# Query and key products with both parts of x in 512 columns, and other places for a loop's margin and a residual

## The chip, the cores and the metric

One core of a Trainium2 chip runs the whole kernel. The metric is the device time of one execution in microseconds, taken as the median of several runs. Durations of single instructions come from one profiled execution. TensorE multiplies, VectorE and ScalarE work on tiles, GpSimd makes masks and constants, and SyncE issues all loads and stores.

## The reference

One decoder layer works on 256 tokens of 2048 features in float32. Attention comes first: `qkv = x @ w_qkv` (2048 x 6144), 16 heads of 128, a causal softmax with a distance penalty over the one block of 256 keys, then `o @ w_o`. The sum `ALPHA * x + attention` goes through a LayerNorm. Then comes a mixture of 32 experts in four groups: each token takes one group and two experts of it, `silu(x @ w_gate) * (x @ w_up)`, weighted, and `@ w_down` (512 hidden features per expert). A second residual sum and a LayerNorm end the layer:

```
x = layer_norm(ALPHA * x + moba_attention(x, w_qkv, w_o), ln1)
x = layer_norm(ALPHA * x + hierarchical_moe(x, ...), ln2)
```

Only one key block exists at this length, so the selection of past blocks adds nothing. The expert weights are 32 x 3 matrices of 4 MB; the kernel reads all of them.

## The kernel before, in words

**Numbers.** For the query, key, value and output products each float32 operand is split in a high part, rounded to the format fp32r, and the rest as a low part. A product is the sum of high x high, high x low and low x high. `transpose_x` turns two chunks of 128 features of x over TensorE into PSUM, and ScalarE copies them to `xh` as the high part, VectorE subtracts to make `xl`. `split_w` does the same for half of a loaded weight tile: ScalarE rounds (L152), VectorE subtracts (L153). Three slots hold split weights, in turn.

**Attention.** `project(g)` makes q, k and v of four heads, `head` the softmax and the values of one head. In q and k the weights of a head are the stationary operand and 256 columns of `xh` or `xl` stream past them; `mm3` writes the three products into the head's half of a PSUM bank (L162 to L164). In v, x is stationary and 512 weight columns stream. A part loads four tiles of 1 MB into a ring of seven slots. After the part, two PSUM banks of 512 columns are copied out, q with the factor 1/sqrt(128) on VectorE (L198), k and v on ScalarE (L200, L202). Two pairs of banks alternate. Only the first part, q of group 0, has its order on TensorE, ScalarE and VectorE written out by hand (`first_order`); behind it the framework orders these engines, and it sets the heads of group g among the products of group g + 1. The first loads on SyncE's queue are a block of x (512 features, two loads) and a tile of weights in turn.

**Experts.** TensorE and SyncE follow the program's order here, and so do the others. Experts go in pairs p = 0 to 15, with up to 64 tokens each. In a pair `first_products` makes gate and up products for one expert after the other, in eight groups of 16 products (`gate_up`, four per expert); after each group `used` gives back two weight slots and issues the next loads into free slots (`advance`), and `between(p, i)` adds small jobs. Then `gather` picks the next pair's tokens, and `second_products` makes the down products in PSUM banks 4 to 7 (`yb`). The rows of pair p are added to the accumulator `acc` in `between` of pair p + 1, groups 0 to 3, over the same four banks (`rest`). Eighteen weight slots are in turn; the order of loads is pair by pair, gate and up (16 MB), then down (8 MB). The last pairs differ: the down weights of pair 14 come after the gate and up weights of pair 15, and those of pair 15 come last, by columns. SyncE waits at each load for one of eight DMA semaphores and for its slot.

**The loop.** After pair `LOOP_AFTER = 10` comes `further_passes`, a loop that serves experts with more than 64 tokens; its count is read from the data and is zero for this input, but all engines meet at its entry (L621) and its exit. Ahead of it, pair 10 keeps `LOOP_SLOTS = 4` slots free for the loop's body; behind it, `advance` fills all free slots.

**The residual.** `residual(n)` adds ALPHA times the normalised x, times gain plus bias, to 512 columns of `acc`. It runs in pair `RES_AT = 12`, once after each of groups 4 to 7 (counted from 0). `rows_of` spreads a vector over the partitions with four small products, into a bank of `mb`, which holds two; three such rows are needed per visit: the gain for either half of the tokens, which VectorE multiplies in place, and the bias.

Of the kernel before, what the change touches and what calls it, by code (L numbers as in the profile page):

```python
# [9 lines left out]
F32 = mybir.dt.float32  # L10
F32R = mybir.dt.float32r
# [3 lines left out]
ALU = mybir.AluOpType  # L15
AX = mybir.AxisListType

P = 128
D = 2048
NT = 2  # L20
NCH = D // P
# [34 lines left out]
def hybrid_kernel(ctx: ExitStack, tc: tile.TileContext, x, w_qkv, w_o, ln1_g, ln1_b, w_grp, b_grp,  # L56
# [68 lines left out]
    nc.scalar.activation(warm, zeros[:, 0:1], AF.Exp)  # L125


    xh = [slot(s, [P, 8, 256], f"xh{i}", F32R) for i, s in enumerate(S_XH)]
    xl = [slot(s, [P, 8, 256], f"xl{i}", F32R) for i, s in enumerate(S_XL)]
    tb = Rot([4, 5, 6, 7])  # L130

    def transpose_x(c2):
        pt = bank(tb(), [P, 2, 256], f"xt{c2}")
        for cc in range(2):
            for tt in range(NT):
                c = 2 * c2 + cc
                nc.tensor.transpose(pt[:, cc, tt * P:(tt + 1) * P], xs[tt][:, c * P:(c + 1) * P], ident)
        i, k = divmod(2 * c2, 8)
        nc.scalar.copy(xh[i][:, k:k + 2, :], pt)
        nc.vector.tensor_sub(xl[i][:, k:k + 2, :], pt, xh[i][:, k:k + 2, :].bitcast(F32))  # L140


    ws = Rot(S_WS)

    def split_w(wt, half, name, pieces=1):

        nch, width = wt.shape[1:]
        t = slot(ws(), [P, 2, nch // 2, width], name, F32R)
        src = wt[:, half * nch // 2:(half + 1) * nch // 2, :]
        for i in range(pieces):  # L150
            c = slice(i * nch // 2 // pieces, (i + 1) * nch // 2 // pieces)
            nc.scalar.copy(t[:, 0, c], src[:, c])  # L152
            nc.vector.tensor_sub(t[:, 1, c], src[:, c], t[:, 0, c].bitcast(F32))  # L153
        return t

    accb = Rot([0, 1, 2, 3])
# [4 lines left out]
    def mm3(dst, ah, al, bh, bl, start, stop, **kw):  # L161
        nc.tensor.matmul(dst, ah, bh, start=start, stop=False, **kw)  # L162
        nc.tensor.matmul(dst, ah, bl, start=False, stop=False, **kw)  # L163
        nc.tensor.matmul(dst, al, bh, start=False, stop=stop, **kw)  # L164

    def first_order():
        return tc.manual_schedule(engines={mybir.EngineType.Activation, mybir.EngineType.DVE, mybir.EngineType.PE})

    def project(g):
        qk = slot(S_QK[g % 2], [P, 2, 4, 256], f"qk{g}")  # L170
        v = vall[:, g % 2]
        for part in range(3):
            with first_order() if g == part == 0 else nullcontext():
                ps = [bank(accb(), [P, 512], f"pj{g}_{part}_{i}") for i in range(2)]
                if g == part == 0:
                    transpose_x(0)
                for j in range(4):
                    wt = first[j] if g == 0 and part == 0 else load_w(w_qkv, j, part * D + g * 512, 512, f"w{g}_{part}_{j}")
                    for half in range(2):
                        w2 = split_w(wt, half, f"ws{g}_{part}_{j}_{half}", 2 if g == part == j == 0 else 1)  # L180
                        if g == part == 0 and (j, half) != (3, 1):
                            transpose_x(2 * j + half + 1)
                        for cc in range(2):
                            c = 4 * j + 2 * half + cc
                            i, k = divmod(c, 8)
                            st, sp = c == 0, c == NCH - 1
                            if part < 2:
                                for hh in range(4):
                                    w = w2[:, :, cc, hh * P:(hh + 1) * P]
                                    mm3(ps[hh // 2][:, (hh % 2) * 256:(hh % 2 + 1) * 256], w[:, 0], w[:, 1], xh[i][:, k, :],  # L190
                                        xl[i][:, k, :], st and hh % 2 == 0, sp and hh % 2 == 1, skip_group_check=True)
                            else:
                                for tt in range(NT):
                                    t = slice(tt * P, (tt + 1) * P)
                                    mm3(ps[tt], xh[i][:, k, t], xl[i][:, k, t], w2[:, 0, cc, :], w2[:, 1, cc, :], st, sp)
            for i in range(2):
                if part == 0:
                    nc.vector.tensor_scalar_mul(qk[:, 0, 2 * i:2 * i + 2, :].rearrange("p a b -> p (a b)"), ps[i], SCALE)  # L198
                elif part == 1:
                    nc.scalar.copy(qk[:, 1, 2 * i:2 * i + 2, :].rearrange("p a b -> p (a b)"), ps[i])  # L200
                else:
                    nc.scalar.copy(v[:, i, :], ps[i])  # L202
        return qk, v

    sb = Rot([4, 5])
# [381 lines left out]
    def residual(n):  # L587

        cs = slice(n * 512, (n + 1) * 512)
        for tt in range(NT):  # L590
            g_ = rows_of(0, n, mb(), f"g1_{n}_{tt}")
            g4 = g_.rearrange("p (a c) -> p a c", c=4)
            nc.vector.scalar_tensor_tensor(g4, xn[tt][:, n].rearrange("p c a -> p a c"), ALPHA, g4, op0=ALU.mult, op1=ALU.mult)  # L593
            nc.vector.tensor_add(acc[tt][:, cs], acc[tt][:, cs], g_)  # L594
        b_ = rows_of(1, n, mb(), f"b1_{n}")
        for tt in range(NT):
            nc.vector.tensor_add(acc[tt][:, cs], acc[tt][:, cs], b_)

    def gates():
# [75 lines left out]

    def first_products(p):

        keep = LOOP_SLOTS if p == LOOP_AFTER else 0
        gu = [bank(gub(), [P, 512], f"gu{p}_{i}") for i in range(2)]
        hs = sm.tile([P, 512], F32, name=f"hs{p}", tag="ptv")  # L680
        for side in range(2):
            e = 2 * p + side
            for j in range(4):
                gate_up(gu[side], side, lambda c: xg[:, c, side], j, held["g", e, j], held["u", e, j])
                used(("g", e, j), ("u", e, j), keep=keep)
                between(p, 4 * side + j)
            if side == 0:
                o2_next = onehots(p + 1) if p + 1 < NP else None
                ot, gs = slots_of(p, o2, gatef[:, :, 2 * p:2 * p + 2])
            hidden(gu[side], side, gs, hs)  # L690
        return hs, ot, o2_next

    def second_products(p, ht):
        y = [bank(yb[n], [P, 512], f"y{p}_{n}") for n in range(4)]
        for k in range(4):
            for n in range(4):
                for side in range(2):
                    nc.tensor.matmul(y[n][sides[side]], ht[:, k, sides[side]], held["d", 2 * p + side, k][:, n * 512:(n + 1) * 512],  # L698
                                     start=k == 0, stop=k == 3, skip_group_check=True)
            used(("d", 2 * p, k), ("d", 2 * p + 1, k), keep=LOOP_SLOTS if p == LOOP_AFTER else 0)  # L700
        return y

    def between(p, i):

        nonlocal gatef
        if p == 0 and i < 2:
            for c2 in (2 * i + 4, 2 * i + 5):
                gather(c2, xg, o2, 0)
        if p == 0 and i == 1:
            gatef = gates()  # L710
            count_passes()
        if i < 4 and rest is not None:
# [187 lines left out]
```

## Time and profile before

| | us |
|---|---|
| median of three runs (1388.09 to 1393.47) | 1391.52 |
| profiled execution | 1390.78 |
| its span, first to last instruction | 1389.0 |
| TensorE busy | 1332.3 (96%) |
| VectorE busy | 462.7 (33%) |
| ScalarE busy | 334.7 (24%) |

The mean granted clock of TensorE is 0.986. Attention with its output product reaches to about 420 us, the experts from there to about 1350. Busy time of TensorE is modelled and overlaps from product to product, so the distance between starts tells more than a duration. A row of the page's second part has 40 slices of 34.7 us. In groups of instructions the number after the busy time is the mean of one in ns, then comes idle time ahead and what ended it. In a timeline the columns are start, duration, engine, line, operation, operands and count, with the idle time ahead in brackets. The chain of waits has start, duration, engine, tile, line and count.

### The profile page before, as it was taken

To read this page: it belongs to the slowest core of one execution; us is meant where nothing else is said; L and a number is where in the kernel's file an instruction comes from. 1 tells how busy PE (TensorE), PEld (TensorE's weight loads), DVE (VectorE), ACT (ScalarE), POOL (GpSimd) and SP (SyncE) were. 2 spreads that over 40 slices of the span, in tenths; PEclk is the share of its full clock that TensorE was granted. 3 is DMA by queue.
4 is the path that set the end of the run, shared out by engine and by line. 5 is a ranking of instruction groups with operands and counts; after the bars stand their busy time and mean duration, and the time that the engine had idled before them with its cause. 6 is when DMAs were issued, how large, how long until landed. Compare 5 with 4: busy or idle time off the path is not lost. (4 is left out here: it accounts for less than half of the span.)

```text
span 1389.0 us, 17892 instructions
## 1 busy us (share of the span) xinstructions
PE 1332.3 (96%) x7497; PEld 795.8 (57%) x7497; DVE 462.7 (33%) x814; ACT 334.7 (24%) x566; POOL 19.4 (1%) x58
## 2 busy tenths in 40 slices
PE   8999999999999999999999999999996997999996
PEld 8999898988896434534434344343443443443432
DVE  4454545545443122221221212212122026222146
ACT  4353534445334101101111011010111010111132
POOL 1000120000000000000000000000000000000000
PEclk9999999999999999999999999999998998999998
DMA  9745446477549899999999999999999999999992
GB/s 342 243 152 182 152 153 206 158 243 272 176 176 367 358 423 420 421 421 421 421 422 421 420 421 421 422 421 421 421 421 420 421 420 422 407 414 420 420 371 61
DMA packets 103015, 475.50 MB, mean 342 GB/s; under 512 B 12756, under 2 KB 18964, under 8 KB 54804
## 3 DMA queue, kind: packets, MB, share of 16 engines
q1 hardware_dynamic: 102932, 474.33, 86.3%
q8 instruction: 60, 0.98, 0.3%
q14 instruction: 23, 0.19, 0.0%
HBM read 472.20 MB, written 2.10 MB: 341 GB/s over the span
## 5 line engine op out<-in xcount | busy, mean ns | idle before, releaser
L543 PE MATMUL gu<-wg,xg 128*64 128x512 f32 x1024 | 460.4, 599 | 12.4 <-PEq L621 12.4
L543 PE MATMUL gu<-wu,xg 128*64 128x512 f32 x1024 | 460.9, 600 | 5.2 <-DMA wu<-in_moe_w_up_dram 5.2
L543 PEld LDWEIGHTS gu<-wg,xg 128*64 128x64 f32 x1024 | 135.2, 138 | 242.3 <-issue 235.3
L698 PE MATMUL y<-wd,ht 128*64 128x512 f32 x960 | 209.5, 594 | 0.8 <-ACT ht L555 0.8
L543 PEld LDWEIGHTS gu<-wu,xg 128*64 128x64 f32 x1024 | 135.1, 138 | 48.7 <-issue 37.4
L153 DVE TENSOR_TENSOR ws<-w,ws 128x1024 fp32r<-128x1024 f32 x88 | 108.2, 1230 | 121.7 <-ACT ws L152 121.7
L162 PE MATMUL pj<-xh,ws 128*128 128x256 f32 x512 | 147.1, 287 | 0.8 <-ACT ws L152 0.8
L164 PE MATMUL pj<-xh,ws 128*128 128x256 f32 x512 | 146.5, 287 | 1.0 <-DVE ws L153 1.0
L163 PE MATMUL pj<-xl,ws 128*128 128x256 f32 x512 | 146.8, 287 | 0.0
L510 PE MATMUL pg<-o,xn 128*128 128x128 f32 x1024 | 134.1, 286 | 11.8 <-ACT xg L519 6.1
L698 PEld LDWEIGHTS y<-wd,ht 128*64 128x64 f32 x960 | 68.7, 137 | 131.0 <-issue 127.1
L510 PEld LDWEIGHTS pg<-o,xn 128*128 128x128 f32 x1024 | 123.2, 195 | 33.3 <-issue 14.5
L576 DVE TENSOR_TENSOR acc<-acc,cb 128x512 f32<-128x512 f32 x112 | 71.9, 683 | 165.9 <-PE cb L566 165.9
L152 ACT CAST ws<-w 128x1024 fp32r<-128x1024 f32 x88 | 92.4, 1050 | 135.6 <-PE pj L164 131.1
L559 ACT CAST ys_all<-y 128x512 fp32r<-128x512 f32 x60 | 35.2, 586 | 282.9 <-PE y L698 154.7
L164 PEld LDWEIGHTS pj<-xh,ws 128*128 128x128 f32 x512 | 98.7, 193 | 1.7 <-DVE ws L153 1.6
L162 PEld LDWEIGHTS pj<-xh,ws 128*128 128x128 f32 x512 | 98.8, 193 | 1.4 <-ACT ws L152 1.2
L560 DVE TENSOR_TENSOR ys_all<-y,ys_all 128x512 fp32r<-128x512 f32 x60 | 41.3, 688 | 173.6 <-ACT ys_all L559 171.6
L163 PEld LDWEIGHTS pj<-xl,ws 128*128 128x128 f32 x512 | 98.8, 193 | 0.1
L548 DVE SCALAR_TENSOR_TENSOR hs<-hs,gs,gu 64x512 f32<-64x512 f32 x32 | 23.9, 747 | 205.1 <-ACT hs L547 203.8
L519 ACT ACTIVATE xg<-pg,gbp 128x128 f32<-128x128 f32 x128 | 51.6, 453 | 104.4 <-PE pg L510 104.4
L517 DVE TENSOR_SCALAR xg<-pg,gbp 128x128 f32<-128x128 f32 x128 | 46.7, 406 | 85.1 <-PE pg L510 84.9
(218 smaller groups left out, 1225.6 us busy)
## 6 DMA issues: line engine op xcount, KB each, us to landing
wg<-in_moe_w_gate_dram SPq DMA_DIRECT2D x128, 1024.0 KB, 19.8
wu<-in_moe_w_up_dram SPq DMA_DIRECT2D x128, 1024.0 KB, 19.8
wd<-in_moe_w_down_dram SPq DMA_DIRECT2D x120, 1024.0 KB, 19.8
w<-in_attn_w_qkv_dram SPq DMA_DIRECT2D x44, 1024.0 KB, 5.2
wow<-in_attn_w_o_dram SPq DMA_DIRECT2D x16, 1024.0 KB, 5.2
wl<-in_moe_w_down_dram SPq DMA_DIRECT2D x6, 1024.0 KB, 14.3
wfirst<-in_attn_w_qkv_dram SPq DMA_DIRECT2D x3, 1024.0 KB, 10.1
xs<-in_x_dram SPq DMA_DIRECT2D x8, 256.0 KB, 8.7
```

The source lines that it names most:

```text
L152: nc.scalar.copy(t[:, 0, c], src[:, c])
L153: nc.vector.tensor_sub(t[:, 1, c], src[:, c], t[:, 0, c].bitcast(F32))
L162: nc.tensor.matmul(dst, ah, bh, start=start, stop=False, **kw)
L163: nc.tensor.matmul(dst, ah, bl, start=False, stop=False, **kw)
L164: nc.tensor.matmul(dst, al, bh, start=False, stop=stop, **kw)
L510: nc.tensor.matmul(pg[:, cc], xn[tt][:, n, c, :], o2[:, tt].rearrange("p e s -> p (e s)"), start=tt == 0, stop=tt == 1)
L517: nc.vector.tensor_scalar(to, pg[:, cc], g_, b_, op0=ALU.mult, op1=ALU.add)
L519: nc.scalar.activation(to, pg[:, cc], AF.Identity, scale=g_, bias=b_)
L543: nc.tensor.matmul(gu[to], xg(4 * j + c), w[:, c, :], start=st, stop=sp, skip_group_check=True)
L560: nc.vector.tensor_sub(ys[0:rows, 1, 0:width], y[0:rows, 0:width], ys[0:rows, 0, 0:width].bitcast(F32))
L576: nc.vector.tensor_add(t, t, cb)
L698: nc.tensor.matmul(y[n][sides[side]], ht[:, k, sides[side]], held["d", 2 * p + side, k][:, n * 512:(n + 1) * 512], start=k == 0, stop=k == ...
```

## The change

In q and k, `xt` holds the high and the low part of a chunk of x side by side, 2 x 256 columns. The high weights of a head meet all 512 columns in one product, the low weights the 256 high columns in a second one. The results of both halves are summed when they leave PSUM: ScalarE copies one half, VectorE adds the other. A pass has two heads (256 weight columns, two loads of 1 MB) in place of four, and two passes make a part. The factor of q goes into the split of its weights. v keeps its products. The first loads are reordered accordingly.

`LOOP_KEEP = 10` slots stay free ahead of the loop in place of four, of which the loop's body still gets four. The residual goes to pairs 11 and 12, after groups 4 and 6 of each, and its rows go to three of the banks `yb`.

```diff
-RES_AT = 12
+RES_AT = (11, 12)
 LOOP_SLOTS = 4
+LOOP_KEEP = 10
...
-    for j in range(4):
-        load_x(j)
-        first.append(load_w(w_qkv, j, 0, 512, f"wfirst{j}", pieces=4 if j == 0 else 1))
+    for j in range(2):
+        load_x(2 * j)
+        first.append(load_w(w_qkv, j, 0, 256, f"wfirst{j}", pieces=4 if j == 0 else 2))
+        load_x(2 * j + 1)
...
+    xt = [slot(s, [P, 4, 2, 256], f"xt{i}", F32R) for i, s in enumerate(S_XH + S_XL)]
...
+        hi = xt[i][:, k:k + 2, 0]
+        nc.scalar.copy(hi, pt)
+        nc.vector.tensor_sub(xt[i][:, k:k + 2, 1], pt, hi.bitcast(F32))
...
+                nc.scalar.mul(t[:, 0, c], src[:, c], factor)
+                nc.vector.scalar_tensor_tensor(t[:, 1, c], src[:, c], factor, t[:, 0, c].bitcast(F32), op0=ALU.mult,
+                                               op1=ALU.subtract)
...
+        for part in range(2):
+            for pair in range(2):
+                start = g == part == pair == 0
+                with first_order() if start else nullcontext():
+                    ps = [bank(accb(), [P, 2, 256], f"pj{g}_{part}_{pair}_{i}") for i in range(2)]
+                    if start:
+                        for c2 in range(2):
+                            transpose_x(c2)
+                    for j in range(2):
...
+                        for half in range(2):
+                            w2 = split_w(wt, half, f"ws{g}_{part}_{pair}_{j}_{half}", 2 if start and j == 0 else 1,
+                                         None if part else SCALE)
+                            if start and (j, half) != (1, 1):
+                                for c2 in range(2):
+                                    transpose_x(4 * j + 2 * half + 2 + c2)
+                            for cc in range(4):
+                                c = 8 * j + 4 * half + cc
+                                x2 = xt[c // 4][:, c % 4]
+                                for i in range(2):
+                                    w = w2[:, :, cc, i * P:(i + 1) * P]
+                                    nc.tensor.matmul(ps[i], w[:, 0], x2, start=c == 0, stop=False, skip_group_check=True)
+                                    nc.tensor.matmul(ps[i][:, 0], w[:, 1], x2[:, 0], start=False, stop=c == NCH - 1,
+                                                     skip_group_check=True)
+                for i in range(2):
+                    to = qk[:, part, 2 * pair + i, :]
+                    nc.scalar.copy(to, ps[i][:, 1])
+                    nc.vector.tensor_add(to, to, ps[i][:, 0])
...
-        for tt in range(NT):
-            g_ = rows_of(0, n, mb(), f"g1_{n}_{tt}")
-            g4 = g_.rearrange("p (a c) -> p a c", c=4)
+        g_ = [rows_of(0, n, yb[tt], f"g1_{n}_{tt}") for tt in range(NT)]
+        b_ = rows_of(1, n, yb[2], f"b1_{n}")
+        for tt in range(NT):
+            g4 = g_[tt].rearrange("p (a c) -> p a c", c=4)
...
-        keep = LOOP_SLOTS if p == LOOP_AFTER else 0
+        keep = LOOP_KEEP if p == LOOP_AFTER else 0
...
-        if p == RES_AT and i >= 4:
-            residual(i - 4)
+        if p in RES_AT and i in (4, 6):
+            residual(2 * RES_AT.index(p) + (i - 4) // 2)
```

## Rows read from the trace of the kernel before

**Rows 1.** The page's second part, 40 slices: TensorE busy in tenths, loads in GB/s
```profile
PE   8999999999999999999999999999996997999996
...
GB/s 342 243 152 182 152 153 206 158 243 272 176 176 367 358 423 420 421 421 421 421 422 421 420 421 421 422 421 421 421 421 420 421 420 422 407 414 420 420 371 61
```
**Rows 2.** Windows: stretch, length, busy us per engine, granted clock, DMA share, GB/s
```profile
172.00:174.00 2.00, 0.62 (x6) 0.45 (x5) 1.28 (x2) 1.04 (x1) 2.00 (x4) 1.00 0.00 0
...
176.00:178.00 2.00, 2.00 (x10) 2.00 (x10) 1.36 (x2) 0.00 (x0) 1.87 (x3) 0.50 0.00 0
```
**Rows 3.** Timeline of TensorE: key products, then value products
```profile
109.88 0.28 PE L162 MATMUL pj<-xh,ws 128*128 128x256 f32 x1
...
110.72 0.28 PE L163 MATMUL pj<-xl,ws 128*128 128x256 f32 x1
...
290.66 0.39 PE L163 MATMUL pj<-ws,xh 128*128 128x512 f32 x1
...
292.02 0.39 PE L163 MATMUL pj<-ws,xh 128*128 128x512 f32 x1
```
**Rows 4.** Groups of instructions by shape, VectorE
```profile
L153 DVE TENSOR_TENSOR ws<-w,ws 128x1024 fp32r<-128x1024 f32 x88 | 108.2, 1230 | 121.7 <-ACT ws L152 121.7
...
L593 DVE SCALAR_TENSOR_TENSOR g<-xn,g 128x512 f32<-128x512 f32 x8 | 8.2, 1030 | 8.4 <-PE g L583 8.4
...
L233 DVE TENSOR_TENSOR otl<-o,oth 128x256 fp32r<-128x256 f32 x16 | 6.7, 421 | 2.9 <-ACT oth L232 2.9
```
**Rows 5.** Timeline of the first 60 us, TensorE and VectorE
```profile
11.84 0.55 PE L137 MATMUL xt<-ident,xs 128*128 128x128 f32 x3 [0.37 <-DMA xs<-in_x_dram]
...
36.06 1.41 DVE L198 TENSOR_SCALAR qk<-pj 128x512 f32<-128x512 f32 x2 [0.69 <-PE pj L164]
```
**Rows 6.** Loads of the output projection's weights from 330 us on
```profile
L85 SPq DMA_DIRECT2D wow<-in_attn_w_o_dram x6: 367/368/379, 334.3 to 364.6; - x6
...
DMA to landing us min/median/max: 5.0/5.2/5.6
```
**Rows 7.** Timeline around the loop, SyncE's loads and TensorE
```profile
1052.01 0.33 SPq L409 DMA_DIRECT2D wu<-in_moe_w_up_dram  x1
...
1066.92 0.33 SPq L409 DMA_DIRECT2D wu<-in_moe_w_up_dram  x1
...
1076.19 1.08 PE L543 MATMUL gu<-wg,xg 128*64 128x512 f32 x1 [12.45 <-PEq L621]
```
**Rows 8.** Line 621, the loop: sequencers, ns min/median/max, first and last start
```profile
L621 SPq EVENT_SEMAPHORE  x26: 17/17/17, 1067.8 to 1076.1; - x26
...
L621 DVEq EVENT_SEMAPHORE  x8: 21/21/21, 1064.5 to 1076.1; - x8
...
L621 PEldq COMPARE_BRANCH  x2: 97/3064/6030, 1069.3 to 1069.5; - x2
```
**Rows 9.** DMA issues: count, KB each, median us from issue to landing
```profile
wu<-in_moe_w_up_dram SPq DMA_DIRECT2D x128, 1024.0 KB, 19.8
...
gb<-in_ffn_ln_g_dram SPq DMA_DIRECT2D x1, 8.0 KB, 1.5
```
**Rows 10.** Chain of waits in pair 12, groups 4 and 5, then the gather
```profile
1149.17 3.58 PE gu L543 x16
...
1155.33 5.28 PE gu L543 x16
...
1176.84 7.45 PE pg L510 x40
```
**Rows 11.** Chain of waits near the end: down products of pair 14
```profile
1332.86 13.73 PE y L698 x64
```
**Rows 12.** Down weights issued from 1318 to 1322 us, the last of pair 14
```profile
L409 SPq DMA_DIRECT2D wd<-in_moe_w_down_dram x2: 327/355/383, 1318.3 to 1318.7; - x2
...
DMA to landing us min/median/max: 12.0/13.1/14.1
```
**Rows 13.** Windows, columns as in rows 2, five microseconds behind the loop
```profile
1190.00:1195.00 5.00, 5.00 (x26) 1.72 (x24) 0.00 (x0) 0.00 (x0) 0.00 (x0) 1.00 0.81 316
```

More of the change, by code (lines that the diff above doesn't have):

```diff
@@ L125, in hybrid_kernel @@
     nc.scalar.activation(warm, zeros[:, 0:1], AF.Exp)
-    xh = [slot(s, [P, 8, 256], f"xh{i}", F32R) for i, s in enumerate(S_XH)]
-    xl = [slot(s, [P, 8, 256], f"xl{i}", F32R) for i, s in enumerate(S_XL)]
+    xt = [slot(s, [P, 4, 2, 256], f"xt{i}", F32R) for i, s in enumerate(S_XH + S_XL)]
     tb = Rot([4, 5, 6, 7])
@@ L137, in transpose_x, with split_w @@
                 nc.tensor.transpose(pt[:, cc, tt * P:(tt + 1) * P], xs[tt][:, c * P:(c + 1) * P], ident)
-        i, k = divmod(2 * c2, 8)
-        nc.scalar.copy(xh[i][:, k:k + 2, :], pt)
-        nc.vector.tensor_sub(xl[i][:, k:k + 2, :], pt, xh[i][:, k:k + 2, :].bitcast(F32))
+        i, k = divmod(2 * c2, 4)
+        hi = xt[i][:, k:k + 2, 0]
+        nc.scalar.copy(hi, pt)
+        nc.vector.tensor_sub(xt[i][:, k:k + 2, 1], pt, hi.bitcast(F32))
     ws = Rot(S_WS)
-    def split_w(wt, half, name, pieces=1):
+    def split_w(wt, half, name, pieces=1, factor=None):
         nch, width = wt.shape[1:]
@@ L151, in split_w @@
             c = slice(i * nch // 2 // pieces, (i + 1) * nch // 2 // pieces)
-            nc.scalar.copy(t[:, 0, c], src[:, c])
-            nc.vector.tensor_sub(t[:, 1, c], src[:, c], t[:, 0, c].bitcast(F32))
+            if factor is None:
+                nc.scalar.copy(t[:, 0, c], src[:, c])
+                nc.vector.tensor_sub(t[:, 1, c], src[:, c], t[:, 0, c].bitcast(F32))
+            else:
+                nc.scalar.mul(t[:, 0, c], src[:, c], factor)
+                nc.vector.scalar_tensor_tensor(t[:, 1, c], src[:, c], factor, t[:, 0, c].bitcast(F32), op0=ALU.mult,
+                                               op1=ALU.subtract)
         return t
@@ L171, in project @@
         v = vall[:, g % 2]
[L172 to L192, printed above, removed]
-                                for tt in range(NT):
[L194 to L202, printed above, removed]
@@ new lines, in project @@
+        for part in range(2):
[7 more added lines that the diff above has]
+                    for j in range(2):
+                        wt = first[j] if start else load_w(w_qkv, j, part * D + g * 512 + pair * 256, 256,
+                                                           f"w{g}_{part}_{pair}_{j}")
+                        for half in range(2):
[16 more added lines that the diff above has]
+                    nc.vector.tensor_add(to, to, ps[i][:, 0])
@@ new lines, in project @@
+        ps = [bank(accb(), [P, 512], f"pv{g}_{i}") for i in range(2)]
+        for j in range(4):
+            wt = load_w(w_qkv, j, 2 * D + g * 512, 512, f"wv{g}_{j}")
+            for half in range(2):
+                w2 = split_w(wt, half, f"wvs{g}_{j}_{half}")
+                for cc in range(2):
+                    c = 4 * j + 2 * half + cc
+                    x2 = xt[c // 4][:, c % 4]
+                    for tt in range(NT):
+                        t = slice(tt * P, (tt + 1) * P)
+                        mm3(ps[tt], x2[:, 0, t], x2[:, 1, t], w2[:, 0, cc, :], w2[:, 1, cc, :], c == 0, c == NCH - 1)
@@ L203, in project @@
+        for i in range(2):
+            nc.scalar.copy(v[:, i, :], ps[i])
         return qk, v
@@ L589, in residual @@
         cs = slice(n * 512, (n + 1) * 512)
+        g_ = [rows_of(0, n, yb[tt], f"g1_{n}_{tt}") for tt in range(NT)]
+        b_ = rows_of(1, n, yb[2], f"b1_{n}")
         for tt in range(NT):
-            g_ = rows_of(0, n, mb(), f"g1_{n}_{tt}")
-            g4 = g_.rearrange("p (a c) -> p a c", c=4)
+            g4 = g_[tt].rearrange("p (a c) -> p a c", c=4)
             nc.vector.scalar_tensor_tensor(g4, xn[tt][:, n].rearrange("p c a -> p a c"), ALPHA, g4, op0=ALU.mult, op1=ALU.mult)
-            nc.vector.tensor_add(acc[tt][:, cs], acc[tt][:, cs], g_)
-        b_ = rows_of(1, n, mb(), f"b1_{n}")
-        for tt in range(NT):
+            nc.vector.tensor_add(acc[tt][:, cs], acc[tt][:, cs], g_[tt])
             nc.vector.tensor_add(acc[tt][:, cs], acc[tt][:, cs], b_)
@@ L699, in second_products @@
                                      start=k == 0, stop=k == 3, skip_group_check=True)
-            used(("d", 2 * p, k), ("d", 2 * p + 1, k), keep=LOOP_SLOTS if p == LOOP_AFTER else 0)
+            used(("d", 2 * p, k), ("d", 2 * p + 1, k), keep=LOOP_KEEP if p == LOOP_AFTER else 0)
         return y
```

## The prediction

> **What bounds the kernel now.** I read the 40 slices of the page first. TensorE is at 9 tenths in nearly every slice; the loads move 152 to 272 GB/s in slices 3 to 12 and about 421 from slice 15 on [rows 1]. So there are two regimes. Up to about 420 us TensorE alone sets the pace, and the loads have room. The windows show it waiting around 173 us, and after that wait busy without a gap at the lower of its clock levels, 1.2 GHz, a granted 0.50 [rows 2]. From about 490 us to the further_passes loop the stream of expert weights is full, so what the attention part gains arrives there whole. At the loop this changes: SyncE issues its last load ahead of it at 1066.92, all engines meet there, and TensorE starts again at 1076.19 after 12.45 us of idling [rows 7]. From there to the end the chain of waits runs over TensorE, while the loads go on arriving. The last down-projection weights of pair 14 land at 1318.7 + 14.1 = 1332.8 us [rows 12]; TensorE begins those products only at 1332.86 and needs 13.73 us [rows 11]. With the weights there earlier, it would need the last quarter, 3.4 us, after that landing. So behind the loop TensorE is about 10 us late against its loads, and the loop and residual edits can give back this much, unless they move the loads.
>
> **Query and key products.** Per chunk of x and head there were three products of 256 columns; now one has 512 and one 256. Consecutive products start 7 steps in 0.84 us apart at 256 columns and 6 steps in 1.36 us at 512, so 0.120 and 0.2267 us [rows 3]; the slope is 0.4167 ns per column and the constant 13.3 ns. The pair costs 0.3467 in place of 0.360 us, one constant less. There are 16 chunks x 16 heads x 2 = 512 of them: 6.8 us. The two widths in alternation don't occur in the trace. Bounds: two constants gone, 0.333, and nothing gained, 0.360; so 13.7 to 0 us. I take 6.8, the sum of the two rows, since each product still loads its own weights, as in both rows.
> The Trainium skill (TensorE: Matmul & The Clock Gate, Back-to-back issue gap) gives an isolated product at the full clock its columns plus about 2.5 ns. One product less would then save 512 x 2.5 ns = 1.3 us, an estimate. The rows have 13.3 ns at either width, and so speak against it here.
>
> **What hides beside them.** The weight splits keep number and size, 1.23 us each on VectorE [rows 4]. For the queries the subtraction becomes a scalar_tensor_tensor: 1.23 if it goes as the subtraction does, 2.06 if as the one at 1.03 per 512 [rows 4]. I take the first, since the second reads with a stride. Either fits beside the 8 x 0.3467 = 2.77 us that TensorE spends on what one split delivers. Four evacuations of 512 per group of heads become eight copies and eight adds of 256; an add is near 0.42 [rows 4], 3.4 us of VectorE in some 80. Passes alternate between two pairs of banks, so an evacuation has a whole pass, 11.1 us, as cover; without it, each pass would end in a wait of up to a copy and an add, 0.8 us. These weights now come in rows of 1 KB in place of 2. Of six output-projection loads the last four had such rows, and all landed within 5.0 to 5.6 us [rows 6], so I cost this at nothing; twice as long is still hidden by seven slots.
>
> **The start.** Two transposed pairs of chunks now stand ahead of the first products on TensorE, and behind these two more, which need the second block of x. That block keeps its place behind 1.5 MB of other loads: before, the transposes of its second half began at 11.84 us, and three took 0.55 with the run-out of the last [rows 5]. Seven more take about 1 us, so the products begin at 12.8. First pass: 32 x 0.3467 = 11.1, and 16 further transposes, 2.0: it ends at 25.9, and the second at 37.0. Before, the same products ended at 36.06 [rows 5]: 0.9 us later now. TensorE will also have idled some 5 us. A shorter idle was followed by the lower clock [rows 2], so I expect it here; the price of one such stretch is taken from a group of 16 products right after a wait, 5.28 in place of 3.58 us [rows 10], 1.7. The other 448 pairs gain 6.0. Attention: 6.0 - 0.9 - 1.7 = 3.4 us. Bounds: -2 (lower clock twice as long, the pairs gaining half) to 8 (x lands sooner, no fall).
>
> **The residual.** It sat in four places of pair 12. Each bias row waited for one of two banks, which VectorE had to free: from 1149.17 to 1176.84 us TensorE did four groups of 3.58 [rows 10], so 13.3 us were row products, waits and low clock. Now there are four visits in pairs 11 and 12, after groups 5 and 7, in banks of y, which are free there. Twelve small products stay, under 1 us per visit. VectorE's part of one visit is 2 x 1.03 and four adds of half a split, 4 x 0.62, so 4.5 us [rows 4], and lies beside 7.2 us of expert products between visits; at a pair's second visit the hidden product queues behind it on VectorE, less than 1 us. Gain for TensorE: 13.3 - 4 = 9 us.
>
> **The loop.** Of 18 slots in turn, 14 were filled ahead of the loop and now 8 are: six loads fewer on SyncE's queue there. The last is the one of 1052.01 [rows 7]. SyncE's first event at the loop was at 1067.8, VectorE's at 1064.5 [rows 8], after TensorE's last product. So the exit moves 3.3 us ahead, to 1072.9; what stays is TensorE's branch of 6.03 us [rows 8]. The price: the stream ends at 1052.01 + 19.8 = 1071.8, and new data comes some 1.5 us after an issue, as the small load does [rows 9], at 1074.4, a break of 2.6 us that was not there. Bounds: no break (the branch is quicker once the DMA engines drain) and 6 us (the exit stays at 1076.2).
>
> **The sum behind the loop.** TensorE gains 3.3 + 9 = 12.3 us. The loads lose 2.6, and win back the 5 us at 1190 in which they moved 316 in place of 421 GB/s, as TensorE had freed slots late [rows 1, 13]: 1.25. The last weights of pair 14 land at 1332.8 + 1.35 = 1334.2, the products end 3.4 later, at 1337.6, which is 9.0 us ahead of 1332.86 + 13.73 = 1346.6; what follows keeps its length. TensorE's own 12.3 leave 3 us of reserve, so the loads bind. Bounds: 5.6 (break of 6) to 11.6 (none).
> Total: 3.4 + 9.0 = 12.4. The profiled execution took 1390.8 us (span 1389.0), so 1378.4; it lies 0.7 under the median of the three runs: 1379.
>
> **Rivals.**
> 1. The products gain nothing: TensorE waits 0.2 us at each of 32 pass changes, which eats 6.4. For it: 12 changes have become 32 and more, on banks that ScalarE and VectorE must both clear. Against it: at 9 tenths throughout [rows 1], TensorE shows no waits at the 12. 1385.
> 2. The exit stays at 1076.2, the break is 6 us: 1382.5. Against it: TensorE idles from 1063.74 and VectorE is there at 1064.5, so SyncE was the late one [rows 7, 8].
> 3. No break at the loop and no lower clock at the start, 2.6 + 1.7 and some of the 0.9: 1374.
> 4. The 13.3 ns belong to what surrounds a product, and four fifths stay with the pair: 0.3575 us, 5.5 us of the gain missing, 1384.5. The Trainium skill's rule above (TensorE: Matmul & The Clock Gate) leaves a product as little.
> 5. Slower: with eight loads ahead the stream runs dry, and from then on each microsecond of a later exit is one at the end. The place is TensorE's branch, where it waits for what comes next. It decides from an exit at 1072.9 + 12.4 = 1085.3 on, two more such waits; with three, at 1091, 1397. For it: the one of 6.03. Against it: the second branch in that row took 0.097.
> A residual that still stalls TensorE is none: up to 3 us vanish in the reserve.
>
> **How the numbers follow.** Forecast 0.57 (its own range 1375 to 1382), then 0.14, 0.08, 0.12, 0.04 and 0.05 for the rivals in their order. The range 1372 to 1385 leaves out rival 5, half of rival 1 and the edges. Under 0.5%, 7 us, counts as no change, so faster is below 1384.5: 0.57 + 0.08 + 0.12 + 0.04 and a third of rival 1, 0.86; no change 0.09; slower 0.05.
>
> **What would show it.** Right: products of a pair in 0.3467 us; the first ones near 12.8 us at a granted clock below 1; 9 us of idle at the loop, a dip of the DMA rate right behind it and none at 1190; an even pace of the expert groups in pairs 11 and 12; pair 14's last products waiting for their weights. Wrong: TensorE waiting for ScalarE or VectorE between passes, an exit from the loop not tied to SyncE, or an end that doesn't follow pair 14.

## The result and the profile after

| | before | after |
|---|---|---|
| median of 5 runs (lowest to highest), us | 1391.52 (1388.09 to 1393.47) | 1381.11 (1379.51 to 1381.94) |
| profiled execution, us | 1390.78 | 1381.28 |
| its span, us | 1389.0 | 1379.6 |
| first expert product starts, us | 430.74 | 427.65 |
| last weights of pair 14 landed, us | 1332.8 | 1333.65 |
| output products of pair 14 end, us | 1346.6 | 1337.34 |

The ratio of after to before is 0.9933, with a 95% interval of 0.9917 to 0.9949: faster, by 10.4 us of the medians. The forecast was 1379, its own range 1375 to 1382. The first expert product, from which intervals are counted below, stands in these rows of TensorE's timeline, before and after:

```profile
430.74 0.64 PE L543 MATMUL gu<-wg,xg 128*64 128x512 f32 x1
```

```profile
427.65 0.64 PE L564 MATMUL gu<-wg,xg 128*64 128x512 f32 x1
```

Next is the second part of the page of after, TensorE and the rate of the loads (for [rows 1]):

```profile
PE   8999999999999999999999999999997999999986
...
GB/s 324 251 150 191 162 154 213 155 285 232 182 175 367 355 424 420 421 421 421 421 421 421 421 420 421 422 420 420 421 421 378 392 420 421 421 420 421 421 407 149
```

The dip of slices 35 and 36 before (407, 414) is gone; a deeper one (378, 392) has come at slices 31 and 32, at the loop. The next view is the timeline of ScalarE, the copies that close passes of query and key products, the second to fourth of group 0 and then the first three of group 2:

```profile
37.80 0.73 ACT L209 COPY qk<-pj 128x256 f32<-128x256 f32 x2 [1.42 <-PE pj L205]
49.11 0.72 ACT L209 COPY qk<-pj 128x256 f32<-128x256 f32 x2 [1.42 <-PE pj L205]
60.42 0.72 ACT L209 COPY qk<-pj 128x256 f32<-128x256 f32 x2 [1.43 <-PE pj L205]
...
178.37 0.72 ACT L209 COPY qk<-pj 128x256 f32<-128x256 f32 x2 [4.48 <-PE pj L205]
189.46 0.72 ACT L209 COPY qk<-pj 128x256 f32<-128x256 f32 x2 [1.38 <-PE pj L205]
200.55 0.72 ACT L209 COPY qk<-pj 128x256 f32<-128x256 f32 x2 [1.38 <-PE pj L205]
```

A pass has 32 pairs of products. In group 0 it takes 11.31 us, so 0.3533 per pair; in group 2 it takes 11.09, so 0.3467, the forecast's figure. Groups 1 and 3, not shown, have 11.31. One code, two paces. ScalarE waits for TensorE in every row, not the other way round. The groups of VectorE, the subtraction of a split and the addition of an evacuation, in mean ns:

```profile
L160 DVE SCALAR_TENSOR_TENSOR ws<-w,ws 128x1024 fp32r<-128x1024 f32 x28 | 34.3, 1225 | 20.3 <-ACT ws L159 20.2
...
L210 DVE TENSOR_TENSOR qk<-qk,pj 128x256 f32<-128x256 f32 x32 | 12.4, 421 | 10.4 <-ACT qk L209 10.4
```

Both as forecast from [rows 4], 1.23 and 0.42 us. The start, in the timeline of TensorE (for [rows 5]) and in windows:

```profile
9.44 0.48 PE L139 MATMUL xt<-ident,xs 128*128 128x128 f32 x1 [2.62 <-DMA xs<-in_x_dram]
10.16 1.76 PE L139 MATMUL xt<-ident,xs 128*128 128x128 f32 x7 [0.24 <-DMA xs<-in_x_dram]
11.56 0.78 PE L204 MATMUL pj<-xt,ws 128*128 128x512 f32 x1
```

```profile
10.00:15.00 5.00, 4.84 (x18) 4.36 (x19) 2.58 (x4) 2.22 (x4) 0.00 (x0) 0.50 1.06 364
...
15.00:20.00 5.00, 5.00 (x32) 4.44 (x32) 2.29 (x3) 2.04 (x3) 0.00 (x0) 0.94 1.10 350
```

TensorE stood for 2.62 us before the second block of x, began the products at 11.56, and ran them at a granted 0.50, 1.2 GHz, up to 15 us. Next the loop: SyncE's last load ahead and first behind, TensorE's restart (for [rows 7]), its branch (for [rows 8]) and the windows around it, with the one of [rows 13] last:

```profile
1048.89 0.33 SPq L430 DMA_DIRECT2D wu<-in_moe_w_up_dram  x1
1069.38 0.34 SPq L430 DMA_DIRECT2D wg<-in_moe_w_gate_dram  x1
...
1069.37 1.09 PE L564 MATMUL gu<-wg,xg 128*64 128x512 f32 x1 [8.74 <-PEq L641]
```

```profile
L641 PEldq COMPARE_BRANCH  x2: 97/3094/6090, 1062.4 to 1062.6; - x2
```

```profile
1060.00:1065.00 5.00, 0.62 (x3) 0.19 (x2) 1.29 (x2) 0.54 (x2) 0.00 (x0) 0.85 0.87 364
1065.00:1070.00 5.00, 0.63 (x2) 0.32 (x4) 0.52 (x2) 0.00 (x0) 0.56 (x5) 0.50 0.29 111
1070.00:1075.00 5.00, 5.00 (x17) 1.57 (x15) 0.00 (x0) 0.00 (x0) 0.15 (x5) 0.62 0.89 300
1075.00:1080.00 5.00, 5.00 (x26) 1.87 (x24) 0.00 (x0) 0.00 (x0) 0.00 (x0) 1.00 1.00 398
...
1190.00:1195.00 5.00, 5.00 (x24) 1.84 (x22) 1.89 (x3) 0.59 (x1) 0.00 (x0) 1.00 1.01 421
```

TensorE idles 8.74 us in place of 12.45, and its branch takes 6.09 of them. Between SyncE's two loads lie 20.5 us; the last load ahead landed 19.9 us after its issue, so the stream ran dry. Against 421 GB/s the four windows at the loop lack (57 + 310 + 121 + 23) x 5 / 421 = 6.1 us of the stream. Pair 12 in the chain of waits (for [rows 10]), and the end of pair 14 (for [rows 11, 12]):

```profile
1144.67 3.58 PE gu L564 x16
1148.25 0.55 PE g L604 x8
1148.81 0.22 PE b L604 x4
1149.03 7.02 PE gu L564 x32
...
1161.41 0.75 DVE hs L569
```

```profile
1313.75 19.90 DMA wd<-in_moe_w_down_dram
...
1333.69 3.65 PE y L718 x14
```

The residual's rows now cost TensorE 0.8 us at a visit and no group is stretched. From the first expert product of pair 12 to that of pair 13 it is 58.5 us, before 72.4. At the end the chain no longer runs over TensorE but over the loads: the last 14 products of pair 14 begin as its last weights have landed.

### The profile page after: what moved, and what is told of

The parts are those of the page before. It is cut to its first block, busy times and chain, and to the rows that moved or that the text cites. A ratio compares the mean times of both kernels' runs of the same rounds, so it can differ in the third digit from the quotient of the medians.

```text
span 1379.6 us, 16921 instructions
## 1 busy us (share of the span) xinstructions
PE 1327.4 (96%) x6985; PEld 766.6 (56%) x6985; DVE 470.5 (34%) x838; ACT 340.6 (25%) x590; POOL 18.6 (1%) x58
## 5 line engine op out<-in xcount | busy, mean ns | idle before, releaser
L204 PE MATMUL pj<-xt,ws 128*128 128x512 f32 x512 | 184.3, 402 | 0.0
L205 PE MATMUL pj<-xt,ws 128*128 128x256 f32 x512 | 146.9, 287 | 0.0
L204 PEld LDWEIGHTS pj<-xt,ws 128*128 128x128 f32 x512 | 97.1, 190 | 22.2
L205 PEld LDWEIGHTS pj<-xt,ws 128*128 128x128 f32 x512 | 97.6, 191 | 0.5 <-DVE ws L160 0.2
L568 ACT ACTIVATE hs<-gu 64x512 f32<-64x512 f32 x32 | 18.9, 592 | 206.9 <-PE gu L564 206.5
L170 PE MATMUL wo<-wos,oth 128*128 128x512 f32 (+1 forms) x160 | 56.8, 355 | 0.0
L172 PE MATMUL wo<-wos,otl 128*128 128x512 f32 (+1 forms) x160 | 56.5, 353 | 0.0
L171 PE MATMUL wo<-wos,oth 128*128 128x512 f32 (+1 forms) x160 | 55.8, 349 | 0.0
## 6 DMA issues: line engine op xcount, KB each, us to landing
wg<-in_moe_w_gate_dram SPq DMA_DIRECT2D x128, 1024.0 KB, 19.8
wu<-in_moe_w_up_dram SPq DMA_DIRECT2D x128, 1024.0 KB, 19.8
wd<-in_moe_w_down_dram SPq DMA_DIRECT2D x120, 1024.0 KB, 19.8
```

The lines of the kernel that those rows point to most:

```text
L204: nc.tensor.matmul(ps[i], w[:, 0], x2, start=c == 0, stop=False, skip_group_check=True)
L205: nc.tensor.matmul(ps[i][:, 0], w[:, 1], x2[:, 0], start=False, stop=c == NCH - 1, skip_group_check=True)
```

## The experiments

Twelve kernels ran, each beside the kernel before. In the expectations, margin is the number of slots kept free ahead of the loop (10 in the changed kernel, 4 before).

**Parts of the change.** The first four take it apart. The changed products with the old residual, function and call, and the old margin:

```diff
 # against the changed kernel
-RES_AT = (11, 12)
-LOOP_KEEP = 10
+RES_AT = 12
+LOOP_KEEP = 4
...
```

> The changed products and start alone; loop margin 4 and the residual in pair 12 as before. My theory (the products and the start bring the experts forward by 3.1 us, and behind the loop TensorE binds as it did before): 3 us faster than before, ratio 0.998, with loads full at the loop and the idle of 12 us there. Rival (most of the gain is the products, and the loop and residual edits only shift waits): 8 to 10 us faster.

Measured: 1385.83 us, before 1390.3, ratio 0.9968 (0.9955 to 0.998): 4.5 us of gain (2.8 to 6.3 by the interval), the 3.4 of the forecast or a little more, and not the loss of rival 1. In the profiled executions only 2.4 us of it lie ahead of the first expert product (428.39 against 430.74). The last products of pair 14 start 2.5 us earlier counted from there, and 1.9 of these come from pair 12 (70.5 us for 72.4), whose code is the same: the kernel before made the gather behind it at a granted 0.58 from 1175 to 1180 us, this run at 1.00. So part of the 4.5 may not be the products'. Then loop and residual, function and call as in the change, on the old products:

```diff
 # against the kernel before
-RES_AT = 12
+RES_AT = (11, 12)
+LOOP_KEEP = 10
...
```

> Loop margin 10 and the residual in pairs 11 and 12, with the products and the start as before. My theory: 6 to 7 us faster than before, ratio 0.9955; the last weights of pair 14 land about 4 us later, counted from the start of the experts, than before, and its last products wait for them. Rival (TensorE's own gain of 12 us behind the loop counts): 12 us faster.

Measured: 1384.09, ratio 0.9953 (0.9939 to 0.9967), as expected: 6.2 us. The residual without the loop, and the loop without the residual, came later, when the margin was in doubt:

```diff
 # residual alone: as the one above, but
-LOOP_KEEP = 10
+LOOP_KEEP = 4
...
 # loop alone, against the kernel before (both places)
-keep=LOOP_SLOTS if p == LOOP_AFTER else 0
+keep=10 if p == LOOP_AFTER else 0
```

> The kernel before with the new residual alone (four steps in two pairs, their banks among those of the outputs); products, first loads and the margin of 4 at the loop as before. Theory (the margin of 10 breaks the loads and the break costs all that the earlier exit gives and more, once the residual no longer holds TensorE behind the loads): the loads stay unbroken, the output of pair 14 waits for its last load instead of ending 9 us behind it, and the time is about 10 us below before, 1380.3 us, less than the 1384.1 us of loop and residual together. Rival (the exit is worth what was forecast, about 3 us, also with the new residual): 1386 to 1387 us, slower than loop and residual together.

> The kernel before with the margin of 10 at the loop alone; products and residual as before. Theory: TensorE leaves the loop 3.7 us earlier, the loads break and land about 4.4 us later from there on, but with the old residual TensorE ends 9 us behind them, so that the break is hidden and the time follows TensorE: 1390.3 - 3.7 = 1386.6 us. Rival (the break costs also here): 1390 to 1391 us. Last, by the forecast's own terms (3.3 us earlier, 1.25 us of it won back anyway): 1388 us.

Measured: residual alone 1379.28, ratio 0.9926 (0.9912 to 0.9939), before 1390.0 in this comparison; loop alone 1385.47, ratio 0.9973 (0.996 to 0.9985). The larger margin is worth 4.5 us by itself (more than the 3.7 expected), the residual 10.7. The residual's places and its banks were changed together; which of the two ended the waits was not tried. Added to the residual it takes time away: the ratio goes from 0.9926 to 0.9953. The rows of TensorE's restart and of pair 14's last products, first of the residual alone, then of the loop alone, show how:

```profile
1075.19 1.09 PE L544 MATMUL gu<-wg,xg 128*64 128x512 f32 x1 [12.40 <-PEq L621]
...
1331.84 3.65 PE y L698 x14
```

```profile
1073.72 1.09 PE L543 MATMUL gu<-wg,xg 128*64 128x512 f32 x1 [8.77 <-PEq L621]
...
1328.82 13.73 PE y L698 x64
```

With the residual alone TensorE waits its 12.4 us at the loop, the loads never stop (413 to 423 GB/s from 1060 to 1075 us), and pair 14 ends with them (a quarter, 3.65 us, behind the last landing). With the loop alone the break is there as well, but TensorE, held up by the old residual, runs all 64 products in one piece and ends at 1342.55; its last weights had landed at 1337.1, 905.2 behind the first expert product. There the break is hidden and the earlier exit counts.

**The margin.** Three more values in the changed kernel (4 as below, 6 and 8), that kernel again, and a margin of 6 with the residual left out:

```diff
-LOOP_KEEP = 10
+LOOP_KEEP = 4
...
 # residual left out (with a margin of 6)
-            residual(2 * RES_AT.index(p) + (i - 4) // 2)
+            pass
```

> The changed kernel, but 4 slots kept ahead of the loop, as before. Loads-bind theory: the break in the stream (4.4 us at a landing) is gone, TensorE leaves the loop 3.7 us later; the last weights of pair 14 land near 1329 us, TensorE is then the later one by about 2 us; 2 us faster than the changed kernel, about 1379. Rival (what pays is TensorE's earlier exit from the loop): 3.7 us slower than the changed kernel, about 1385.

> The changed kernel with 6 slots kept. SyncE then issues its last load ahead of the loop before VectorE gets there, so the exit is as early as with 10, while four more loads are under way across the loop. Loads-bind theory: no break and the early exit, 4 to 5 us faster than the changed kernel, about 1376.5, loads at 420 GB/s right through the loop. Rival (only the exit counts, the break is hidden): same as the changed kernel, 1381.

> The changed kernel itself once more (margin 10), so that the margins stand beside it in one comparison: 1381 us, with the break in the loads at 1063 to 1075 us and an output of pair 14 that waits 5 us in all for its loads. All theories expect the same of it.

> The changed kernel with a margin of 8 instead of 10. With 6, the last load ahead was issued 10.4 us before TensorE left the loop, with 10 it was 20.5 us, and a load in a full stream takes 19.8 us from issue to landing; with 8 the gap is some 15.5 us. Theory A (the stream stays whole as long as a load is under way): no break, the time of the margin of 6, 1378 us. Theory B (the rate falls already when the last loads are spread over fewer engines, as it did from 1063 us, 6 us before the last landing; and the first new load needs 10 us to land): a partial break of 1 to 2 us, 1379.5 us. If it is as slow as the margin of 10 (1381), the length of the gap is not what matters.

> The changed kernel with a margin of 6, its residual left out altogether (eight products of 128 columns to a bank, six banks for each of the four steps, and the additions on VectorE). Theory (with unbroken loads the stream of weights alone sets the end, the new residual is hidden behind it): no change against the margin of 6 with its residual, 1378 us, the output of pair 14 waits longer for its last load, that lands as late as before. Rival (TensorE is still the bound in places, and each of the four steps costs its 3.6 us or a part of it): 1372 to 1376 us.

Measured, with the start of the first expert product, the start of TensorE behind the loop, and the start of pair 14's last products, which is the landing of its last weights:

| kernel | us | ratio (95%) | first expert product | behind the loop | last landing | landing less first product |
|---|---|---|---|---|---|---|
| margin 10 | 1381.11 | 0.9933 (0.9917 to 0.9949) | 427.65 | 1069.37 | 1333.69 | 906.0 |
| margin 10 again | 1380.45 | 0.9924 (0.991 to 0.9938) | 428.20 | 1069.6 | 1333.46 | 905.3 |
| margin 8 | 1377.83 | 0.9906 (0.989 to 0.9922) | 427.60 | 1068.9 | 1329.85 | 902.3 |
| margin 6 | 1378.3 | 0.9916 (0.9901 to 0.9931) | 427.86 | 1069.49 | 1330.36 | 902.5 |
| margin 4 | 1377.33 | 0.991 (0.9896 to 0.9925) | 426.79 | 1072.49 | 1329.06 | 902.3 |
| margin 6, no residual | 1378.45 | 0.9916 (0.9903 to 0.993) | 428.30 | 1069.91 | 1330.83 | 902.5 |
| residual alone (margin 4) | 1379.28 | 0.9926 (0.9912 to 0.9939) | 429.98 | 1075.19 | 1331.84 | 901.9 |
| loop and residual (margin 10) | 1384.09 | 0.9953 (0.9939 to 0.9967) | 428.56 | 1069.94 | 1333.47 | 904.9 |

The last column has two values. In all five kernels with a margin of 4, 6 or 8 it is 901.9 to 902.5; with 10 it is 904.9 to 906.0. The break so costs 2.4 to 4.1 us. The exit from the loop, counted from the first expert product 4.1 us earlier with 6 than with 4, changes nothing. Both expectations missed here: with 4, TensorE was to be 2 us later than its weights, and with 6 the early exit was to give 1376.5. The residual, left out altogether, changes nothing either: in the waits and the chain of that run TensorE just waits longer for the same landing:

```profile
PE y L718 <- DMA wd<-in_moe_w_down_dram: 5.3, 4, 1.3
```

```profile
1310.97 19.82 DMA wd<-in_moe_w_down_dram
...
1330.83 3.65 PE y L718 x14
```

So behind the loop the stream alone sets the end once the residual is out of TensorE's way. The windows of the margins of 6 and of 8, one fence each, show where the stream stays whole:

```profile
1060.00:1065.00 5.00, 0.84 (x4) 0.35 (x2) 1.28 (x2) 0.76 (x2) 0.00 (x0) 0.84 1.02 423
1065.00:1070.00 5.00, 0.51 (x2) 0.33 (x4) 0.51 (x2) 0.00 (x0) 0.43 (x3) 0.50 1.01 415
1070.00:1075.00 5.00, 5.00 (x16) 1.55 (x14) 0.01 (x1) 0.00 (x0) 0.28 (x5) 0.64 1.01 418
```

```profile
1065.00:1070.00 5.00, 1.11 (x4) 0.55 (x6) 0.52 (x2) 0.00 (x0) 0.71 (x7) 0.50 0.92 365
1070.00:1075.00 5.00, 5.00 (x19) 1.59 (x17) 0.00 (x0) 0.00 (x0) 0.00 (x0) 0.70 0.98 390
```

With 8 the gap between SyncE's loads is 15.4 us, less than the 19.8 of a load, and the rate dips already (1 us of the stream, the part of theory B that came true). Yet the last landing is not later, and the time is that of theory A. In time alone, margins 8 and 10 of one comparison differ by 2.6 us with intervals that overlap a little; the landings tell them apart.

**The pace of the products.** With a margin of 6, all four products of a chunk by width:

```diff
-                                for i in range(2):
-                                    w = w2[:, :, cc, i * P:(i + 1) * P]
-                                    nc.tensor.matmul(ps[i], w[:, 0], x2, ...)
-                                    nc.tensor.matmul(ps[i][:, 0], w[:, 1], x2[:, 0], ...)
+                                ws_ = [w2[:, :, cc, i * P:(i + 1) * P] for i in range(2)]
+                                for i in range(2):
+                                    nc.tensor.matmul(ps[i], ws_[i][:, 0], x2, ...)
+                                for i in range(2):
+                                    nc.tensor.matmul(ps[i][:, 0], ws_[i][:, 1], x2[:, 0], ...)
```

> The changed kernel with a margin of 6 at the loop, and the four products of a chunk in the order 512, 512, 256, 256 columns where the changed kernel has 512, 256, 512, 256. In the changed kernel a pair of one 512 and one 256 column product took 0.3533 us in most stretches and 0.3467 us in one (180 to 210 us). Theory: it is the alternation of widths that costs the 6.6 ns; grouped, a pair takes 0.3467 us everywhere, the query and key products get 384 x 0.0067 + 128 x 0.0133 = 4 us shorter at most, and the time is 1376 us (2.3 below the 1378.3 us of the margin of 6 alone; the shift is smaller than the 4 us because the first 210 us are partly bound by loads). Rival: the pace is set by what happened before (TensorE's wait at 173 us), not by the order; then a pair stays at 0.3533 us outside of 180 to 210 us and the time at 1378.3 us. Second rival: two accumulations to two banks in turn cost more at 256 columns, and a pair gets longer than 0.3533 us: 1380 us.

Measured: 1376.01 us, ratio 0.9907 (0.9892 to 0.9923). The ends of passes in group 0 and group 2 of this run, then two of group 0 with the same margin in the changed order:

```profile
37.70 0.65 ACT L210 COPY qk<-pj 128x256 f32<-128x256 f32 x2 [1.63 <-PE pj L206]
48.84 0.65 ACT L210 COPY qk<-pj 128x256 f32<-128x256 f32 x2 [1.63 <-PE pj L206]
...
190.22 0.65 ACT L210 COPY qk<-pj 128x256 f32<-128x256 f32 x2 [1.61 <-PE pj L206]
201.36 0.65 ACT L210 COPY qk<-pj 128x256 f32<-128x256 f32 x2 [1.61 <-PE pj L206]
```

```profile
37.71 0.72 ACT L209 COPY qk<-pj 128x256 f32<-128x256 f32 x2 [1.37 <-PE pj L205]
48.80 0.72 ACT L209 COPY qk<-pj 128x256 f32<-128x256 f32 x2 [1.36 <-PE pj L205]
```

Grouped, the second to fourth pass of all four groups take 11.14 us, 0.348 per pair, apart from one of 12.13 in group 2 at a low clock. In turn, it takes 11.31 or 11.09, and this time the short passes are in group 0, where the changed kernel had the long ones; in the products alone all four groups have the long ones. Neither theory fits alone: in these runs two paces appear with the order in turn only, and something that differs from run to run decides which of them a group gets. In the profiled run the first expert product came at 427.87 against 427.86, and the two differ in the clock: a granted 0.66 here from 175 to 180 us, behind a wait of TensorE, and 1.00 there. That took back what the passes gained. The 2.3 us of the medians come from different comparisons, and the intervals overlap: a gain of the order is likely, not shown.

**The start.** With a margin of 6, later transposes:

```diff
-                            if start and (j, half) != (1, 1):
-                                for c2 in range(2):
-                                    transpose_x(4 * j + 2 * half + 2 + c2)
                             for cc in range(4):
+                                if start and cc == 2 and (j, half) != (1, 1):
+                                    for c2 in range(2):
+                                        transpose_x(4 * j + 2 * half + 2 + c2)
```

> The changed kernel with a margin of 6 at the loop, and in the first pass the transposes of the next two blocks of x two chunks later (after the second of the four chunks of a half instead of ahead of the first). Theory: the first products stood behind the transposes of x block 2, which landed at 9.4 to 10.1 us; TensorE waited 2.6 us for them and ran at the lower clock until about 15.5 us. With the transposes later the first products start at about 9 us instead of 11.56, the granted clock falls for less than half as long, the second pass ends 2 us earlier (35.8 instead of 37.8 us), and the time is 1376.3 us. Rival: the first products then only wait for the next loads of x or for the split of the weights, the second pass ends where it did (37.8 us), and the time stays at 1378.3 us.

Measured: 1379.66, ratio 0.9923 (0.9909 to 0.9936); the theory falls. TensorE's waits of the first 60 us and a window of this run:

```profile
PE pj L204 <- ACT ws L159: 4.0, 3, 2.5
PE xt L139 <- DMA xs<-in_x_dram: 1.1, 2, 0.9
```

```profile
20.00:25.00 5.00, 4.36 (x18) 3.88 (x19) 1.23 (x1) 1.00 (x2) 0.00 (x0) 0.66 1.10 349
```

The products did start early, at 7.81 us, but then waited for the split of their weights, 2.5 us before one at 20.64, and the clock fell there instead. The second pass closed at 39.80 in place of 37.71.

**Both together.** The grouped order with a margin of 4 (`LOOP_KEEP = 4` in that kernel):

> The changed kernel with a margin of 4 and the products in the order 512, 512, 256, 256 columns. If the stream of loads sets the end and not the exit from the loop, the margins of 4 and 6 give the same time, 1376 us as with 6 (1376.0). Rival: the exit 3.7 us later is worth something, 1378 to 1380 us.

Measured: 1375.92, ratio 0.9899 (0.9884 to 0.9914), the last landing at 1328.27, 902.5 behind the first expert product. That product starts at 425.77, at a granted 1.00 from 175 to 180 us, ahead of all runs in the changed order. It is the fastest kernel run, 4.5 us below the changed one in the same comparison, and its exit from the loop lies 1.9 us later than that of the margin of 6 with the same order (1071.20 against 1069.33).

## Why the prediction was right, and where it was not

**The sum.** Of the forecast's 12.4 us, 3.4 were in the attention and 9.0 behind the loop. The spans differ by 9.4: 3.1 in the attention (430.74 to 427.65), 6.2 from there to the end of pair 14's outputs (915.9 to 909.7), and 0.1 to 0.2 in the tail. That the first of these is so near its forecast is partly luck, and so is a share of the second, as the next paragraphs show.

**Attention.** The size held in these two executions, not its parts. The pair of products took 0.3533 us in most groups; half of the forecast gain per pair, between the forecast and rival 4's 0.3575. The sum of the two rows is no rule for it: the same two products take 0.3533 or 0.3467 in turn and 0.348 grouped, and what sets the pace was not found. The start lost 1.7 us and not 2.6: x landed sooner, the products began at 11.56 and not at 12.8, and the low clock came as forecast. From the close of the second pass (36.06 before, 37.80 after) to the first expert product 4.8 us were gained, forecast 6.0. 320 pairs in three groups at 0.3533 and 128 in group 2 at 0.3467 give 3.8 of it.

The rest, some 1 us, goes with a low clock that was there before at 176 us [rows 2]; after, the same stretch is at 1.00:

```profile
176.00:178.00 2.00, 1.56 (x9) 1.19 (x8) 1.90 (x3) 0.00 (x0) 1.87 (x3) 1.00 0.00 0
```

The change did not remove the low clock. From 175 to 180 us the granted clock is 0.66 in the changed kernel's second run, and 1.00 in loop and residual together, which has the old products: there the way from the close (35.30) to the first expert product (428.56) is 1.4 us shorter than before, and the changed kernel gains 3.4 on it. So executions have to be compared at the same clock there. At 1.00 the first expert product starts at 428.56 with the old products (one run) and at 426.79 to 428.39 with the new ones in the changed order (five runs, mean 427.7), apart from the later transposes; at 0.66 to 0.68 it starts at 430.74 and 429.98 with the old ones (431.95 in the loop alone, at 0.50) and at 428.20 and 428.30 with the new ones. That is 0.9 and 2.1 us for the change, where the forecast had 3.4 and this pair of executions 3.1.
The Trainium skill (TensorE: Matmul & The Clock Gate, Back-to-back issue gap) has about 2.5 ns over the columns, for an isolated product at the full clock. A pair's 768 columns at the forecast's 0.4167 ns are 0.320 us, so the runs, in which each product loads its own weights, have 33, 28 or 27 ns over a pair, and none comes near the 5 ns of two such products.

**Evacuations and splits.** Right: 0.42 and 1.23 us, and TensorE shows no wait for them between passes. Rival 1 is out.

**Residual.** The mechanism was right, and the size too, though the one execution before makes it look too small. Pair 12 took 72.4 us from its first product to that of pair 13, without any residual 56.3 (1123.73 to 1180.05), after 58.5; pair 11 took 55.9 against 53.8 without. So TensorE gained 13.9 - 2.1 = 11.8 us, forecast 9. But some 2 us of this are a low clock in the one execution before (a granted 0.58 and 0.74 in the gather, from 1175 to 1185 us): with the same old residual, pair 12 took 70.5 us in the products alone and 69.9 in the loop alone, which leaves 9.4 to 10.0. The queue before the hidden product was there too, at 1161.41 in the chain above; TensorE waited 0.6 us at the gather behind it. None of this reaches the end, since the loads do.

**The loop.** The exit moved as forecast: counted from the first expert product it came 3.7 us earlier, forecast 3.3, and TensorE's branch stayed (6.09 for 6.03). Rival 2's late exit and rival 5's long branch did not come. The step that failed is "The loads lose 2.6, and win back the 5 us at 1190 [...]: 1.25". The last weights of pair 14 were to land 1.35 us later than before, set against the experts' start, and landed 906.0 - 902.1 = 3.9 later, 3.2 in the repeat. The exit's own gain could not make up for it, as the loads end last. Two terms were mis-sized. The break: the rate fell to 364 before the last load had landed, and the restart was slow, 9.7 to 13.5 us from issue to landing for the three loads issued from 1070.97 to 1072.15 us. The 1.5 us of an 8 KB load was no measure for that. The win-back: the residual alone has no break and no dip at 1190 either, and lands at 901.9 against 902.1, so 0.2 and not 1.25. Nor is the dip a mark of the old residual: in the products alone, which has it, the loads moved 411 and 421 GB/s from 1185 to 1195 us. About 2 of the 6.1 us that the stream lacked at the loop don't appear at the end, nor does the 1 us of the margin of 8; where they came back is open.

**What it missed in kind.** Rival 3 had "no break" as a case of luck, with the exit staying early. The runs show that a margin of 4, 6 or 8 gives it, and that with the residual moved the exit is worth nothing. The two edits were costed as gains of TensorE that add, 3.3 + 9, with the loads taking some 3 of them back. By the same terms the residual alone gives 9 without a break, as much as both together; the forecast did not draw this. The loop's gain exists only while TensorE is late, and the residual removed that lateness.

## What to carry to other kernels

Before an edit is costed in microseconds of an engine, see which of engine and stream ends last once the other edits of the same change are in: here 4.5 us for the larger margin alone turned into a loss beside the new residual. A stream of loads should be kept fed across a barrier: compare the gap in its issues with the time from issue to landing (10.4 and 15.4 us against 19.8 cost nothing at the end here, 20.3 to 20.5 cost 2.4 to 4.1 us). A difference that the times barely resolve can be told by one interval in the trace, as the last landing less the first expert product, steady within 0.7 us over five kernels. And one profiled execution can hold a low clock that the next one of the same kernel lacks, so compare the granted clock of a stretch before a difference in it is put down to the change.

## What the runs showed of the hardware that was not expected

Products of 512 and 256 columns in turn run at one of two steady paces, 11.31 or 11.09 us per 32 pairs, from the same instructions in the same kernel; the pace holds for a whole group of heads and differs from group to group and run to run. With equal widths side by side, in two runs, the second to fourth pass of each group take 11.14 to 11.16 at the full clock. What picks the pace was not found.

The fall of TensorE's clock behind a wait comes and goes with the execution: behind a wait of 1.26 us that ended at 175.3 us the changed kernel was granted 1.00 from 175 to 180 us, and in its other profiled execution, behind one of 1.24 us that ended at 174.4, 0.66.

A stream of 1 MB loads doesn't end sharply: with the last one due at 1068.8 us, the rate was down to 364 GB/s in the window from 1060 to 1065 and 111 in the next, and it was still 398 from 1075 to 1080, with new loads issued from 1069.38 on.
